# First FFN's down projection computed token-major with 14 seven-product cases, its result turned back on TensorE

## The chip, the cores and the metric

The kernel runs on one core of one Trainium2 chip. The metric is the device time of one execution in microseconds (us). A core has five engines with a queue each, used here as follows: TensorE (PE) for matrix products and transposes, VectorE (DVE) and ScalarE (ACT) for element-wise work, GpSimd (POOL) for a little of it, and SyncE (SP), whose queue issues nearly all DMAs.

## The reference

A decoder trunk of two layers on 256 tokens of width 2048, all in float32. Layer 0 mixes tokens with a gated MLP and attention into 256 memory tokens; layer 1 with latent attention (keys and values from a shared compressed side that is built from x after layer 0) and memory attention. After each mixer stands the same kind of feed-forward network, and at the end one RMSNorm. What matters here is the feed-forward network and what follows it:

```python
def conv_ffn(h, w_up, cw, cb, w_down):
    a = h @ w_up                                   # (256, 2048) @ (2048, 2 * 5632)
    ap = jnp.pad(a, ((0, 0), (CONV_W - 1, 0), (0, 0)))
    c = sum(ap[:, k:k + S] * cw[k] for k in range(CONV_W)) + cb
    gate, val = c[..., :D_FF], c[..., D_FF:]
    return (jax.nn.silu(gate) * val) @ w_down      # (256, 5632) @ (5632, 2048)

for l in range(2):
    if l == 1:
        kv = rmsnorm(x, g_kv) @ w_kv_a             # needs x after layer 0
        ...
    x = x + jnp.concatenate([main, mo], axis=-1) @ w_out[l]
    x = x + conv_ffn(rmsnorm(x, g_ffn[l]), w_ffn_up[l], conv_w[l], conv_b[l], w_ffn_down[l])
return rmsnorm(x, g_final)
```

## The kernel before, in words

**Products.** A float32 number is held as a rounded part hi and a rest lo, and a product is three matmuls: hi x hi, hi x lo and lo x hi. Weights come by DMA into tiles `raw` of 128x1024 (SP's queue), ScalarE makes `whi`, VectorE `wlo` (lines 117 and 118, with a gain per row lines 122 and 123). Activations are kept feature-major: x is `xT`, 16 blocks of 128 features by 256 tokens, its split the tiles `xhl0` and `xhl1`.

**Feature-major products** (`gemm_fm`, line 162): weights are stationary and the 256 tokens move. Four blocks of 128 output features accumulate in four PSUM banks while chunks of 256 rows of the weight pass; a chunk is 24 matmuls of 256 columns (lines 156, 157, 159). Small steps are hung between chunks as hooks: hook n is issued after chunk n.

**The feed-forward network** (`ffn`, line 820) goes in three parts of 4, 4 and 3 groups of 512 inner features. For each group come an up-projection for the gate and one for the value, then convolution, SiLU and product, whose result goes into `h`. After a part's groups comes its down projection. In layer 0 this is feature-major too: four column groups of `gemm_fm` over 16 or 12 blocks of 128 rows; each result is added to x (line 662), and in the last part split for layer 1 and squared on POOL for the norm (`next_operand`, line 672).

**Token-major, in layer 1 only** (class `Tokens`, line 1309, and `down_phase`, line 741): during the second group, x is turned into tokens by VectorE in blocks of 32x32 and 16 DMAs (`turn`). The down projection then has h stationary and 512 weight columns moving, in two phases of 1024 columns. A pair k of two 128-row blocks is a 2x2 block product (two token halves, two column halves), by eight products plainly, and by seven for the pairs that `FF_FAST` (line 34) lists. These need sums of weight blocks (`fast_pair`, line 717, on VectorE) and of h blocks (lines 874 to 890). The listed pairs are three in each phase of parts 0 and 1 and two in the first phase of part 2, 14 in all. A plain pair is 24 matmuls of 512 columns, a seven-product pair 21 (lines 757 to 759). Such a phase holds eight PSUM banks: e00, e01, e10, e11 for the four results and m1, m5, m6, m7 for shared products. ScalarE copies the latter into `staged` (`between`), VectorE adds the e banks to the tokens `xt` (line 1381), and `combine` (six operations, line 1362) adds the shared products: in the next part's first up group, or, in the last part, after the next phase's first addition.

**Order.** The tile framework schedules each engine's instructions by a simulated timeline and may interleave neighbouring stages on PE; `behind` (line 698) chains weight loads and splits of a down phase in program order. After layer 0, `layer_b` (line 1050) starts with the key projection over the 16 blocks of x with the gains g_kv, and forms the norm of x by one matmul of `ssum` against ones (`rstd_bc`, line 267) in hook 3.

Of the kernel before, what the change touches and what calls it, by code (L numbers as in the profile page):

```python
# [8 lines left out]
F32 = mybir.dt.float32  # L9
F32R = mybir.dt.float32r  # L10
# [63 lines left out]
class Kernel:  # L74
# [666 lines left out]
    def down_phase(self, dn, col, order, fast, lhs, rhs, pool, fp, between, evict, finish, late=0, late_gains=None):  # L741
        mm = self.nc.tensor.matmul
# [25 lines left out]
        for n, k in enumerate(order):  # L768
# [16 lines left out]
            else:  # L785
# [33 lines left out]

    def ffn(self, l, after=None, to_tokens=None, tokens=None):  # L820
        nc, t = self.nc, self.t
# [4 lines left out]
        with self.tc.tile_pool(name=self.uid("ff"), bufs=1) as fp:  # L826
            g0 = 0
            for part, ng in enumerate(FF_GROUPS):
                h = self.ap.tile([P, NB * 512], F32R, tag="big", name=self.uid("h"))
                last = part == len(FF_GROUPS) - 1  # L830
                phases = FF_FAST[ng] if tokens is not None else (((), ()), ((), ()))
                fast = phases[0][0]
                if tokens is None:
                    plain = {k: h[:, 1024 * k : 1024 * (k + 1)] for k in range(2 * ng)}
                else:
                    parts7, o = {}, 0
                    for k in fast:
                        n = 896 if k in phases[1][0] else 1024
                        parts7[k] = h[:, o : o + 2 * n].rearrange("p (s q) -> p s q", s=2)
                        o += 2 * n  # L840
                    places = [h[:, i : i + 1024] for i in range(o, NB * 512 - 1023, 1024)]
                    plain = {}
                    for k in range(2 * ng):
                        if k not in fast:
                            plain[k] = places.pop(0) if places else tokens.place()
                block = lambda b: plain[b // 2][:, b % 2 * 512 : (b % 2 + 1) * 512]
# [11 lines left out]
                for g in range(g0, g0 + ng):  # L858
# [34 lines left out]
                    hooks_g, hooks_v = dict(first) if g == 0 else {}, {}  # L893
                    if to_tokens is not None and g == 1:
                        hooks_v = to_tokens
                    if tokens is not None and part and g == g0:
# [3 lines left out]
                if last and l == 0:  # L900
                    self.new_hl()
                dn = down[g0 * 512 : (g0 + ng) * 512]
                g0 += ng
                if tokens is not None:

                    rhs = lambda k, q: tuple(parts7[k][:, i, q * P : (q + 1) * P] for i in range(2))

                    def lhs(k, tb):
                        if k // 2 in parts7:
                            return rhs(k // 2, ((0, 7), (1, 2))[k % 2][tb])  # L910
                        x = block(k)
                        return x[:, tb * P : (tb + 1) * P], x[:, S + tb * P : S + (tb + 1) * P]

                    self.chain = {}
                    for ph in range(2):
                        tokens.begin(ph, last)
                        self.down_phase(
                            dn, 1024 * ph, phases[ph][1], phases[ph][0], lhs, rhs, tokens.pool, fp, tokens.between, tokens.evict, tokens.finish, late=2 if last and ph else 0, late_gains=tokens.gains if last and not ph else None
                        )
                    continue  # L920
# [129 lines left out]
    def layer_b(self):  # L1050
# [9 lines left out]
        with tc.tile_pool(name="lb", bufs=1) as lb:  # L1060
# [235 lines left out]
    def run(self):  # L1296
        nc, tc, t = self.nc, self.tc, self.t
        self.constants()
        with tc.tile_pool(name="mk", bufs=1) as self.mk:
            self.start()  # L1300
            self.layer_a()
        self.ffn(0, lambda j: self.next_operand(j, None))
        self.layer_b()
        with tc.tile_pool(name="fin", bufs=1) as fin:

            Tokens(self, fin).ffn()


class Tokens:
    def __init__(self, kernel, pool):  # L1310
        self.k, self.nc, self.pool = kernel, kernel.nc, pool
        self.xt = pool.tile([P, 2, D], F32, name="xt")
        self.sums = pool.tile([P, 2, 5], F32, name="fsums")
        self.part, self.r, self.q, self.v = (pool.tile([P, 2], F32, name=n) for n in ("fpart", "froot", "fq", "fv"))
        self.staged = None
        self.waiting = []

    def ffn(self):
        turns = {2 * r: [lambda r=r: self.turn(r)] for r in range(4)}
        self.k.ffn(1, to_tokens=turns, tokens=self)  # L1320

# [9 lines left out]
    def place(self):  # L1331
        k = self.k
        self.n = (getattr(self, "n", -1) + 1) % 3
        if self.n < 2:
            tag, o = (("kT1", 32), ("mv1", 0))[self.n]
            return k.cp.tile([P, 1056], F32R, tag=tag, name=k.uid("h" + tag))[:, o : o + 1024]
        return k.tmp(self.pool, [P, 1040], "hx", 1, F32R)[:, 16:]

# [3 lines left out]
    def begin(self, ph, last):  # L1342
        k = self.k
        self.ph, self.last = ph, last
        if ph == 0:
            self.staged = k.ap.tile([P, 2, 4, 512], F32, tag="xT", name=k.uid("staged"))
            if last:
                self.gb = k.ap.tile([P, 2 * D], F32, tag="xhl0", name="gb")[:, :D]

    def gains(self, n):  # L1350
        c = slice(512 * n, 512 * (n + 1))
        g = self.k.t["g_final"].rearrange("(o d) -> o d", o=1)[:, c].to_broadcast([P, 512])
        self.k.behind(self.nc.sync.dma_start(out=self.gb[:, c], in_=g))

# [19 lines left out]

    def evict(self, tb, half, acc, piece=None, meanwhile=lambda: None):
        k, nc, xt, sums = self.k, self.nc, self.xt, self.sums
        j = 2 * self.ph + half
        c0, n = (0, 512) if piece is None else (256 * piece, 256)
        c = slice(j * 512 + c0, j * 512 + c0 + n)
        o = xt[:, tb, c]  # L1380
        add = lambda o, a: nc.vector.tensor_tensor(o, a, o, ALU.add)
        add(o, acc[:, c0 : c0 + n])
        if not self.last:
            return
        if self.ph == 0 and half == 0 and tb == 0:
            for ph in self.waiting:
                self.combine(ph)
            self.waiting = []
        one = lambda x: x[:, tb : tb + 1]
        part, r, q, v, gb = self.part, self.r, self.q, self.v, self.gb  # L1390
# [7 lines left out]
        if piece == 0:  # L1398
            add(xt[:, tb, j * 512 + 256 : (j + 1) * 512], acc[:, 256:])
        meanwhile()  # L1400
# [54 lines left out]
```

## Time and profile before

| | |
|---|---|
| median of 3 runs | 2041.59 us (2041.4 to 2046.97) |
| profiled execution | 2041.58 us |
| its span, first to last instruction | 2039.9 us |
| granted TensorE clock, mean | 0.999 |
| busy: PE, DVE, ACT, POOL | 99%, 73%, 54%, 7% of the span |
| moved by DMA | 394.68 MB, 193 GB/s on average |

The profile comes from one execution. An engine's busy time counts instructions in flight, and matmuls overlap, so the distance between starts tells more than the duration of one. Rows of groups read: line, engine, operation, out<-in, shape, count | busy us, mean ns of one | idle us of the engine before them, and what ended it. Rows of waits read: who waited <- for whom: us in total, times, longest. Rows in order of time begin with start and length in us.

### The profile page before, as it was taken

To read this page: it belongs to the slowest core of one execution; us is meant where nothing else is said; L and a number is where in the kernel's file an instruction comes from. 1 tells how busy PE (TensorE), PEld (TensorE's weight loads), DVE (VectorE), ACT (ScalarE), POOL (GpSimd) and SP (SyncE) were. 2 spreads that over 40 slices of the span, in tenths; PEclk is the share of its full clock that TensorE was granted. 3 is DMA by queue.
4 is the path that set the end of the run, shared out by engine and by line. 5 is a ranking of instruction groups with operands and counts; after the bars stand their busy time and mean duration, and the time that the engine had idled before them with its cause. 6 is when DMAs were issued, how large, how long until landed. Compare 5 with 4: busy or idle time off the path is not lost.

```text
span 2039.9 us, 39921 instructions
## 1 busy us (share of the span) xinstructions
PE 2028.9 (99%) x16232; PEld 1962.7 (96%) x16232; DVE 1496.1 (73%) x2268; ACT 1110.4 (54%) x1605; POOL 142.5 (7%) x200
## 2 busy tenths in 40 slices
PE   9999999999999999999999999999999999999998
PEld 8989999999999999999999999999988999889996
DVE  6866767777656767557778786776878877888777
ACT  6754744555434555345545675454656555555555
POOL 0000013000000000000043142300000000000000
PEclk9999999999999999999999999999999999999999
DMA  8876566666666666666665634668765766557664
GB/s 252 236 215 184 166 191 192 195 194 192 194 197 193 192 195 195 194 193 195 195 194 180 183 112 162 194 192 208 224 204 176 213 194 196 195 187 213 197 212 143
DMA packets 234253, 394.68 MB, mean 193 GB/s; under 512 B 53902, under 2 KB 61396, under 8 KB 234068
## 3 DMA queue, kind: packets, MB, share of 16 engines
q1 hardware_dynamic: 233876, 391.58, 64.0%
q8 instruction: 127, 2.08, 0.4%
q14 instruction: 58, 0.48, 0.1%
q10 hardware_dynamic: 192, 0.54, 0.1%
HBM read 387.88 MB, written 2.10 MB: 191 GB/s over the span
## 4 chain that ended last, share of the span: by engine, by line
PE 98%; DVE 0%; ACT 0%; DMA 0%; issue 0%; SPq 0%; ACTq 0%
PE ps L156 26%; PE ps L157 26%; PE ps L159 26%; PE ps L758 4%; PE ps L759 4%; PE ps L757 4%; PE ps L188 2%; PE ps L189 2%; PE ps L190 2%; PE ps L523 1%; PE ps L603 0%; PE ps L601 0%; PE ps L602 0%; PE ps L1206 0%; DMA raw<-in_w_mem_kv 0%; PE ps L995 0%
## 5 line engine op out<-in xcount | busy, mean ns | idle before, releaser
L118 DVE TENSOR_TENSOR wlo<-raw,whi 128x1024 fp32r<-128x1024 f32 x572 | 710.3, 1245 | 385.0 <-ACT whi L117 380.4
L117 ACT ACTIVATE whi<-raw 128x1024 fp32r<-128x1024 f32 x572 | 607.0, 1062 | 686.6 <-PE ps L157 584.5
L156 PE MATMUL ps<-xhl,whi 128*128 128x256 f32 x3264 | 762.8, 277 | 0.0
L157 PE MATMUL ps<-xhl,whi 128*128 128x256 f32 x3264 | 761.2, 276 | 0.0
L157 PEld LDWEIGHTS ps<-xhl,whi 128*128 128x128 f32 x3264 | 612.9, 188 | 0.4
L156 PEld LDWEIGHTS ps<-xhl,whi 128*128 128x128 f32 x3264 | 612.7, 188 | 0.4
L159 PE MATMUL ps<-xhl,wlo 128*128 128x256 f32 x3264 | 436.5, 276 | 0.0
L159 PEld LDWEIGHTS ps<-xhl,wlo 128*128 128x128 f32 x3264 | 400.4, 188 | 0.0
L156 PE MATMUL ps<-h,whi 128*128 128x256 f32 x704 | 163.6, 276 | 0.0
L157 PE MATMUL ps<-h,whi 128*128 128x256 f32 x704 | 163.6, 276 | 0.0
L157 PEld LDWEIGHTS ps<-h,whi 128*128 128x128 f32 x704 | 132.0, 188 | 0.0
L156 PEld LDWEIGHTS ps<-h,whi 128*128 128x128 f32 x704 | 131.8, 188 | 0.0
L156 PE MATMUL ps<-mainhl,whi 128*128 128x256 f32 x512 | 119.6, 277 | 0.0
L157 PE MATMUL ps<-mainhl,whi 128*128 128x256 f32 x512 | 119.4, 276 | 0.0
L852 ACT ACTIVATE c<-a,cT 128x256 f32<-128x256 f32 x176 | 99.3, 589 | 6.1 <-DVE a L236 6.0
L707 ACT ACTIVATE whi<-raw 128x1024 fp32r<-128x1024 f32 x63 | 66.0, 1059 | 56.5 <-PE ps L759 24.9
L708 DVE TENSOR_TENSOR wlo<-raw,whi 128x1024 fp32r<-128x1024 f32 x63 | 76.5, 1222 | 26.8 <-ACT whi L707 25.9
L157 PEld LDWEIGHTS ps<-mainhl,whi 128*128 128x128 f32 x512 | 96.0, 188 | 0.0
L156 PEld LDWEIGHTS ps<-mainhl,whi 128*128 128x128 f32 x512 | 95.9, 188 | 0.0
L159 PE MATMUL ps<-h,wlo 128*128 128x256 f32 x704 | 94.1, 276 | 0.0
L758 PE MATMUL ps<-wlo,h 128*128 128x512 f32 (+1 forms) x230 | 88.8, 388 | 0.3 <-DVE wlo L708 0.2
L759 PE MATMUL ps<-whi,h 128*128 128x512 f32 (+1 forms) x230 | 88.9, 387 | 0.0
(373 smaller groups left out, 2703.1 us busy)
## 6 DMA issues: line engine op xcount, KB each, us to landing
raw<-in_w_ffn_up SPq DMA_DIRECT2D x352, 512.0 KB, 3.8
raw<-in_w_ffn_down SPq DMA_DIRECT2D x154, 512.0 KB, 4.8
raw<-in_w_out SPq DMA_DIRECT2D x64, 512.0 KB, 4.6
raw<-in_w_in_a SPq DMA_DIRECT2D x56, 512.0 KB, 4.5
raw<-in_w_mem_kv SPq DMA_DIRECT2D x31, 512.0 KB, 4.7
gate<-in_w_ffn_down SPq DMA_DIRECT2D x22, 512.0 KB, 5.9
raw<-in_w_in_b SPq DMA_DIRECT2D x16, 512.0 KB, 4.5
raw<-in_w_kv_a SPq DMA_DIRECT2D x9, 512.0 KB, 5.1
```

What stands on the lines that cost most here:

```text
L117: nc.scalar.activation(hi[:, :n], raw[:, :n], AF.Copy)
L118: nc.vector.tensor_tensor(lo[:, :n], raw[:, :n], hi[:, :n].bitcast(F32), ALU.subtract)
L156: mm(acc[:, :S], wh, x[:, :S], start=first, stop=False)
L157: mm(acc[:, :S], wh, x[:, S:], start=False, stop=False)
L159: mm(acc[:, :S], wl, x[:, :S], start=False, stop=last)
L188: mm(acc, xh, wh, start=first, stop=False)
L707: self.behind(self.nc.scalar.activation(hi, w, AF.Copy))
L708: self.behind(self.nc.vector.tensor_tensor(lo, w, hi.bitcast(F32), ALU.subtract))
L757: mm(o, xh, wh, start=start, stop=False)
L758: mm(o, xh, wl, start=False, stop=False)
L759: mm(o, xl, wh, start=False, stop=stop)
L852: nc.scalar.activation(c, a, AF.Identity, scale=w(2), bias=w(3))
```

## The change

Layer 0's feed-forward network takes the token-major way of layer 1. The class `Tokens` becomes the base of two: `Last` keeps what layer 1 did, and `Inner` serves layer 0. Per part of layer 0:

- the up-projections write h in the form of layer 1, seven sums of blocks for the listed pairs; x is turned into tokens during the second group of layer 0;
- the down projection runs as two calls of `down_phase` with the same `FF_FAST`;
- in the last part, the two phases' results are added into `xt`, and ScalarE squares every 512 columns of a token half with a running sum (`sums`);
- in the second phase of the last part, hooks 1 to 4 turn the finished blocks 0 to 7 of x back to feature-major: four PE transposes for two blocks into one PSUM bank, ScalarE copies hi into `xhl` and x into a new `xT`, VectorE makes lo;
- blocks 8 to 15 are turned in hooks 1 and 2 of layer 1's key projection, and the hook of the norm's matmul goes from 3 to 4;
- `ssum` is no longer summed by POOL; it is the identity times the token's sum of squares, so that the same matmul with ones gives the same row.

The three places for h outside its tile lie in a pool of their own in layer 0, and the tile `we` of the seven-product pairs, in both layers, takes the buffer `src`.

```diff
@@ class Kernel
     def halves(self):
         tiles = [self.ap.tile([P, NB // 2, 512], F32R, tag=f"xhl{i}", name=self.uid("xhl")) for i in range(2)]
+        self.hl_tiles = tiles
...
-        one = self.tmp(pool, [P, 1040], "we", 1, F32R)[:, :1024]
+        one = self.tmp(pool, [P, 1024], "src", 1, F32R)
...
@@ down_phase, at the end of each pair
+            for f in hooks.get(n, ()):
+                f()
...
@@ ffn
-                phases = FF_FAST[ng] if tokens is not None else (((), ()), ((), ()))
+                phases = FF_FAST[ng]
...
+                self.chain = {}
+                for ph in range(2):
+                    extra = tokens.begin(ph, last)
+                    self.down_phase(
+                        dn, 1024 * ph, phases[ph][1], phases[ph][0], lhs, rhs, tokens.pool, fp, tokens.between, tokens.evict, tokens.finish, **extra
+                    )
+                if last:
+                    tokens.done()
-                for j in range(4):
-                    src = self.rows(dn, j * 512, 512)
-
-                    def ed(b, acc):
-                        self.add_residual(4 * j + b, acc)
-                        if last:
-                            after(4 * j + b)
-
-                    self.gemm_fm(src, list(range(4 * ng)), 4, block, ed)
...
@@ layer_b
-            self.gemm_fm(self.rows(wkv, 0, KR), ks, 4, x, ek, gain=gk, hooks={3: [lambda: self.rstd_bc(rb, ssum, D)]})
+            hooks = self.pending | {4: [lambda: self.rstd_bc(rb, ssum, D)]}
+            self.gemm_fm(self.rows(wkv, 0, KR), ks, 4, x, ek, gain=gk, hooks=hooks)
...
@@ run
-        self.ffn(0, lambda j: self.next_operand(j, None))
+        with tc.tile_pool(name="mid", bufs=1) as mid:
+            Inner(self, mid).ffn(0)
...
 class Tokens:
+    places = ("hx0", 0), ("hx1", 0), ("hx2", 0)
...
+    def added(self, tb, half, acc, c0=0, n=512):
         j = 2 * self.ph + half
+        o = self.xt[:, tb, j * 512 + c0 : j * 512 + c0 + n]
+        self.nc.vector.tensor_tensor(o, acc[:, c0 : c0 + n], o, ALU.add)
+        if self.last and self.ph == 0 and half == 0 and tb == 0:
             for ph in self.waiting:
                 self.combine(ph)
             self.waiting = []
+        return j, o
...
+class Inner(Tokens):
+    def begin(self, ph, last):
+        super().begin(ph, last)
+        return {"hooks": {n: [lambda n=n: self.turned(2 * n - 2)] for n in range(1, 5)}} if last and ph else {}
+
+    def evict(self, tb, half, acc):
+        j, o = self.added(tb, half, acc)
+        if self.last:
+            junk = self.quarters()[:, :512]
+            self.nc.scalar.activation(junk, o, AF.Square, accum_out=self.sums[:, tb, j : j + 1])
+
+    def turned(self, k0):
+        k, nc = self.k, self.nc
+        if k0 == 0:
+            k.new_hl()
+            k.x = k.ap.tile([P, NB, S], F32, tag="xT", name=k.uid("xT"))
+
+        def put(b, acc):
+            a = acc.rearrange("p (k s) -> p k s", k=2)
+            hl = k.hl_tiles[b // 8][:, b % 8 : b % 8 + 2, :]
+            nc.scalar.activation(hl[:, :, :S], a, AF.Copy)
+            nc.vector.tensor_tensor(hl[:, :, S:], a, hl[:, :, :S].bitcast(F32), ALU.subtract)
+            nc.scalar.activation(k.x[:, b : b + 2, :], a, AF.Copy)
+
+        k.token_transpose(self.xt, k0, k0 + 2, put)
+
+    def done(self):
+        k, nc = self.k, self.nc
+        total = self.sums[:, :, 4]
+
+        def squares():
+            nc.vector.tensor_reduce(total, self.sums[:, :, :4], AX.X, ALU.add)
+            for tb in range(2):
+                nc.vector.tensor_scalar(k.ssum[:, tb * P : (tb + 1) * P], k.ident, total[:, tb : tb + 1], None, ALU.mult)
+
+        squares()
+        k.pending = {1 + i: [lambda i=i, j=j: self.turned(8 + 4 * i + 2 * j) for j in range(2)] for i in range(2)}
...
+class Last(Tokens):
+    places = ("kT1", 32), ("mv1", 0), ("hx", 0)
...
```

More of the change, by code (lines that the diff above doesn't have):

```diff
@@ L817, in down_phase, with ffn @@
             finish(1)
-    def ffn(self, l, after=None, to_tokens=None, tokens=None):
+    def ffn(self, l, to_tokens, tokens):
         nc, t = self.nc, self.t
@@ L830, in ffn @@
                 last = part == len(FF_GROUPS) - 1
-                phases = FF_FAST[ng] if tokens is not None else (((), ()), ((), ()))
+                phases = FF_FAST[ng]
                 fast = phases[0][0]
[L833 to L845, printed above, removed]
+                parts7, o = {}, 0
+                for k in fast:
+                    n = 896 if k in phases[1][0] else 1024
+                    parts7[k] = h[:, o : o + 2 * n].rearrange("p (s q) -> p s q", s=2)
+                    o += 2 * n
+                places = [h[:, i : i + 1024] for i in range(o, NB * 512 - 1023, 1024)]
+                plain = {}
+                for k in range(2 * ng):
+                    if k not in fast:
+                        plain[k] = places.pop(0) if places else tokens.place()
                 block = lambda b: plain[b // 2][:, b % 2 * 512 : (b % 2 + 1) * 512]
@@ L893, in ffn @@
                     hooks_g, hooks_v = dict(first) if g == 0 else {}, {}
-                    if to_tokens is not None and g == 1:
+                    if g == 1:
                         hooks_v = to_tokens
-                    if tokens is not None and part and g == g0:
+                    if part and g == g0:
                         hooks_g = tokens.deferred()
@@ L1312, in __init__, with hold, ffn @@
         self.xt = pool.tile([P, 2, D], F32, name="xt")
+        self.held = [self.hold(tag) for tag, _ in self.places]
+        for tag, (owner, n) in [(t, h) for (t, _), h in zip(self.places, self.held)] + [("src", (pool, 1024))]:
+            if owner is pool:
+                pool.tile([P, n], F32R, tag=tag, name=kernel.uid(tag), bufs=1)
         self.sums = pool.tile([P, 2, 5], F32, name="fsums")
-        self.part, self.r, self.q, self.v = (pool.tile([P, 2], F32, name=n) for n in ("fpart", "froot", "fq", "fv"))
-        self.staged = None
         self.waiting = []
-    def ffn(self):
+        self.n = 0
+    def hold(self, tag):
+        return self.pool, 1024
+    def ffn(self, l):
         turns = {2 * r: [lambda r=r: self.turn(r)] for r in range(4)}
-        self.k.ffn(1, to_tokens=turns, tokens=self)
+        self.k.ffn(l, turns, self)
     def turn(self, r):
@@ L1342, in begin @@
     def begin(self, ph, last):
-        k = self.k
         self.ph, self.last = ph, last
         if ph == 0:
[L1346 to L1353, printed above, removed]
+            self.staged = self.k.ap.tile([P, 2, 4, 512], F32, tag="xT", name=self.k.uid("staged"))
+        return {}
     def between(self, accs):
@@ new lines, with __init__, hold, begin @@
+class Last(Tokens):
+    places = ("kT1", 32), ("mv1", 0), ("hx", 0)
+    def __init__(self, kernel, pool):
+        super().__init__(kernel, pool)
+        self.part, self.r, self.q, self.v = (pool.tile([P, 2], F32, name=n) for n in ("fpart", "froot", "fq", "fv"))
+    def hold(self, tag):
+        return (self.pool, 1024) if tag == "hx" else (self.k.cp, 1056)
+    def begin(self, ph, last):
+        super().begin(ph, last)
+        if not last:
+            return {}
+        if ph:
+            return {"late": 2}
+        self.gb = self.k.ap.tile([P, 2 * D], F32, tag="xhl0", name="gb")[:, :D]
+        return {"late_gains": self.gains}
+    def gains(self, n):
+        c = slice(512 * n, 512 * (n + 1))
+        g = self.k.t["g_final"].rearrange("(o d) -> o d", o=1)[:, c].to_broadcast([P, 512])
+        self.k.behind(self.nc.sync.dma_start(out=self.gb[:, c], in_=g))
+    def evict(self, tb, half, acc, piece=None, meanwhile=lambda: None):
+        k, nc, xt, sums = self.k, self.nc, self.xt, self.sums
+        c0, n = (0, 512) if piece is None else (256 * piece, 256)
+        j, o = self.added(tb, half, acc, c0, n)
+        c = slice(j * 512 + c0, j * 512 + c0 + n)
+        if not self.last:
+            return
```

51 lines of the change are left out of this document (16 added, 35 removed).

## The prediction

> **What bounds the kernel now.** I read the page from the top, then the waits of TensorE, then its order of time. The first columns of the page give busy time and share of the span; the chain is the work that ended last, followed back.
>
> ```profile
> span 2039.9 us, 39921 instructions
> PE 2028.9 (99%) x16232; PEld 1962.7 (96%) x16232; DVE 1496.1 (73%) x2268; ACT 1110.4 (54%) x1605; POOL 142.5 (7%) x200
> PEclk9999999999999999999999999999999999999999
> PE 98%; DVE 0%; ACT 0%; DMA 0%; issue 0%; SPq 0%; ACTq 0%
> ```
>
> The chain is 98% PE and the clock is granted in full in every slice. The waits of PE are these, and no others:
>
> ```profile
> PE ps L490 <- DVE ones L287: 1.1, 1, 1.1
> PE ps L523 <- ACT memhl L457: 0.7, 1, 0.7
> PE ps L758 <- DVE wlo L708: 0.2, 1, 0.2
> PE ps L603 <- DVE pT L245: 0.2, 1, 0.2
> ```
>
> They sum to 2.2 us of 2039.9. So the time is the work in PE's queue: a matmul less is time gained, a matmul more is time lost, and work on VectorE, ScalarE or GpSimd counts only if it makes PE wait. What a matmul costs is its distance to the next start, not its 276 or 389 ns of busy time, because they overlap. Two answers in order of time give that distance, for groups of 24 matmuls of 256 columns (rows of the last 8 of each group):
>
> ```profile
> 1074.04 1.07 PE L159 MATMUL ps<-xhl,wlo 128*128 128x256 f32 x8
> 1076.76 1.07 PE L159 MATMUL ps<-xhl,wlo 128*128 128x256 f32 x8
> ```
>
> and for the moving operand of 512 columns in layer 1:
>
> ```profile
> 1512.78 0.39 PE L758 MATMUL ps<-wlo,h 128*128 128x512 f32 x1
> 1513.01 0.39 PE L759 MATMUL ps<-whi,h 128*128 128x512 f32 x1
> 1513.23 0.39 PE L758 MATMUL ps<-wlo,h 128*128 128x512 f32 x1
> 1513.46 0.39 PE L759 MATMUL ps<-whi,h 128*128 128x512 f32 x1
> ```
>
> 2.72 us / 24 = 0.1133 us for 256 columns; (1513.46 - 1512.78) / 3 = 0.227 us for 512. The price is by column, so turning the loop from feature-major to token-major gains nothing by itself. Only leaving out products does.
>
> **The change part by part.** *Removed from PE.* Before, part 0 of layer 0 has 8 pairs of row blocks x 4 column groups x 24 = 768 matmuls of 256 columns. After, it is what layer 1 has already: 2 phases x (5 plain pairs x 24 + 3 seven-product pairs x 21) = 366 of 512. Both can be read as stages of this trace. The first two rows are the start and the last eight matmuls of part 0 in layer 0, the others the start and end of the same part in layer 1:
>
> ```profile
> L156 PE MATMUL ps<-h,whi x704: 276/276/276, 528.2 to 1071.1; 128*128 128x256 f32 x176
> 614.36 1.07 PE L159 MATMUL ps<-h,wlo 128*128 128x256 f32 x8
> 1495.53 0.40 PE L757 MATMUL ps<-whi,h 128*128 128x512 f32 x1
> 1578.77 0.40 PE L759 MATMUL ps<-whi,h 128*128 128x512 f32 x1
> 1579.01 0.28 PE L156 MATMUL ps<-xhl,whi 128*128 128x256 f32 x1
> ```
>
> Layer 0: 614.36 + 8 x 0.1133 - 528.2 = 87.07 us. Layer 1: 1579.01 - 1495.53 = 83.48 us, with four 256-column matmuls of the next stage drawn in between (0.47 us): 83.01 us. Difference 4.06 us, of which 18 omitted products x 0.2267 = 4.08 are the reason; the borders between phases cost nothing visible. Part 1 has the same plan: 4.06 again. Part 2 has two seven-product pairs in its first phase only: 6 x 0.2267 = 1.36. Together 14 cases x 3 = 42 matmuls: **-9.48 us**.
>
> *Added to PE.* Eight groups of four transposes of 128x128. The trace has such groups in the memory tokens at the start, 24 matmuls of 256 columns between one and the next:
>
> ```profile
> L405 PE MATMUL ps<-ident,mtok x32: 272/273/371, 4.4 to 26.7; 128*128 128x128 f32 x32
> 22.76 0.62 PE L523 MATMUL ps<-memhl,whi 128*128 128x256 f32 x4
> 23.21 0.60 PE L405 MATMUL ps<-ident,mtok 128*128 128x128 f32 x4
> 23.57 0.71 PE L523 MATMUL ps<-memhl,whi 128*128 128x256 f32 x4
> 26.39 0.60 PE L405 MATMUL ps<-ident,mtok 128*128 128x128 f32 x4
> ```
>
> From one group to the next it is 3.18 us, 2.72 of them matmuls, so a group costs 0.46 (0.36 until the next matmul starts, and 0.10 that the first one after it is late). 8 x 0.46 = **+3.68 us**. From below, with all switches hidden, 8 x 0.35 = 2.8; from above, one transpose at a time between matmuls:
>
> ```profile
> 211.49 0.27 PE L644 MATMUL ps<-ident,mp 128*128 128x128 f32 x1
> 211.52 0.37 PE L156 MATMUL ps<-xhl,whi 128*128 128x256 f32 x1
> 211.73 0.49 PE L644 MATMUL ps<-ident,mp 128*128 128x128 f32 x3
> ```
>
> 0.24 us for one transpose with one matmul, 0.13 above the matmul: 32 x 0.13 = 4.2. I take the group's price, since the code issues them in fours. The sums of squares cost PE nothing new: one matmul against the ones is there before and after, only one chunk later (hook 4 for hook 3).
>
> [...]
>
> *VectorE and ScalarE in the phases.* Columns of the next rows: length, then busy us and instructions of PE, PEld, DVE, ACT, POOL, then the clock.
>
> ```profile
> 528.10:615.20 87.10, 87.10 (x771) 87.10 (x770) 50.20 (x66) 37.41 (x41) 0.00 (x0) 1.00 0.63 194
> 1495.50:1578.60 83.10, 83.10 (x371) 68.90 (x370) 72.14 (x93) 47.76 (x58) 0.00 (x0) 1.00 0.56 190
> 1600.00:1700.00 100.00, 100.00 (x885) 100.00 (x884) 75.23 (x117) 55.73 (x75) 0.00 (x0) 1.00 0.69 197
> ```
>
> The weight sums of the seven-product pairs take VectorE from 50.2 of 87.1 us to 72.1 of 83.1, and PE is still busy throughout. The third row is up-projection in layer 1, with the seven sums of h and the deferred combination in it: 885 matmuls in 100 us, full speed. I cost all of this at nothing, hidden behind PE; the cover that is left is about 11 us in each part. Without it the extra 22 us of VectorE would show.
>
> *The turn of x into tokens* moves into the second up group of layer 0, with 4 transposes on VectorE and 16 DMAs put into SP's queue among the weight loads:
>
> ```profile
> L1325 DVE STREAM_TRANSPOSE xs<-xT x4: 1240/1242/1246, 1380.1 to 1397.0; 128x1024 f32<-128x1024 f32 x4
> L1329 SPq DMA_DIRECT2D xt<-xs x16: 591/664/5072, 1381.5 to 1409.2; - x16
> ```
>
> In layer 1 the same step stands in that place without a wait of PE. Nothing again; uncovered it would be 5 us of VectorE.
>
> *What leaves* (residual additions, splits, the squares on POOL) was beside PE and gains nothing.
>
> *The last phase and the hand-over.* Here the before kernel has no model, so I count. Durations:
>
> ```profile
> L1381 DVE TENSOR_TENSOR xt<-ps,xt 128x512 f32<-128x512 f32 x23 | 15.3, 685 | 7.0 <-PE ps L759 6.9
> L1397 ACT ACTIVATE fjunk<-xt 128x512 f32<-128x512 f32 x7 | 4.4, 626 | 5.6 <-DVE xt L1381 5.0 <-DVE xt L1362 0.6
> L457 ACT ACTIVATE memhl<-ps 128x512 fp32r<-128x512 f32 x8 | 4.8, 595 | 7.2 <-PE ps L405 7.2
> L458 DVE TENSOR_TENSOR memhl<-ps,memhl 128x512 fp32r<-128x512 f32 x8 | 5.5, 690 | 5.9 <-ACT memhl L457 5.9
> L122 ACT ACTIVATE whi<-raw,gT 128x512 fp32r<-128x512 f32 x96 | 63.9, 716 | 42.6 <-PE ps L157 20.4 <-DMA raw<-in_w_mem_kv 12.8 <-issue 7.8
> L123 DVE SCALAR_TENSOR_TENSOR wlo<-raw,gT,whi 128x512 fp32r<-128x512 f32 x96 | 72.7, 794 | 19.5 <-ACT whi L122 19.5
> 1995.11 0.39 PE L759 MATMUL ps<-we,h 128*128 128x512 f32 x1
> 2004.55 1.22 DVE L1362 TENSOR_TENSOR xt<-xt,staged 128x1024 f32<-128x1024 f32 x1
> ```
>
> The first transposes need the combination of the phase before. In layer 1 it ended at 2005.8, and the last product with the tile we, which closes that phase, started at 1995.11; the hook stands two pairs, 48 x 0.227 = 10.9 us, into the next phase, at 2006.2 on that scale. The cover is 0.4 us, and 0.7 more because layer 0 lacks the multiplication by the final gains that stands in between; four transposes held up there would hold up all of PE behind them. At the end, PE goes into the first four chunks of the key projection, 4 x 2.72 = 10.9 us, with operands turned earlier; the second half of x is needed in chunk 4. ScalarE must do meanwhile four squares (3.3 us with the reads of the sums), eight copies from PSUM (4.8) and the weights (1.43 a chunk, 5.7): 13.8 us against 10.9, plus the 4 us before the end in which the first accumulators are already whole. VectorE: four additions (2.7), four subtractions (2.8), weights (1.6 a chunk, 6.4): 11.9. Both just fit, and four buffers of weights lie ahead. Queued behind a late copy on ScalarE would be the next weights, and PE waits for those. From below nothing; from above the 2.9 us by which ScalarE exceeds the four chunks. I take 0.2, near the other borders of phases.
>
> Sum against the profiled execution of 2041.58 us (span 2039.9 and 1.7 around it; the median of the three runs is 2041.59): 2041.58 - 9.48 + 3.68 + 0.2 = **2036.0 us**.
>
> **The rivals.**
> *Hand-over late.* Copies and squares hold ScalarE and PE waits once or twice, or the first transposes reach PE before the combination is done. For it: the two ledgers above are nearly full. Against: the weights lie ahead. 1.5 to 4 us: 2037.5 to 2040.
>
> *Transposes not pipelined.* If each waits for the one before, 32 x 0.273 = 8.7 us: 2041.0. [...]
>
> *Slower: accumulators.* A seven-product phase holds all eight PSUM banks, and the next phase needs banks that four additions of 0.685 must free. If PE stands at the border until they are done, that is 2.74 us, at five borders and the hand-over 16.4: 2052. It decides for slower from 5.6 / 6 = 0.93 us a border, and for slower by more than 0.3% from 2.0. Layer 1 has the same five borders, and there PE waited 0.2 us in all.
>
> *The products are omitted but PE gains nothing,* because weight sums come late on VectorE and PE runs at its pace: then the transposes alone remain, 2045. Against: part 0 of layer 1 took 83.01 us.
>
> *Transposes hidden* under a 512-column stream, 2.8 us or less: 2034.5 or below. For it only that no group of this trace stands in such a stream.
>
> **How the numbers follow.** The forecast, 2034.5 to 2037.5, has 0.64; late hand-over 0.16; transposes not pipelined 0.04; accumulators 0.07; no gain on PE 0.04; transposes hidden 0.05. The range 2034.5 to 2040.0 holds the first two, 0.80; its ends are also the bounds of the unknown costs (2.8 for the transposes and no wait give 2034.9; 4.2 with a wait of 2.9 gives 2039.2). 0.3% of the median is 6.1 us, about what a measurement of this kernel can tell from no change. Faster by more than that is below 2035.5: the hidden transposes and a quarter of the forecast, 0.22. Slower: the accumulators and a little of the no-gain case, 0.08. The rest, 0.70, lies between: I expect a gain of 0.27%.
>
> **What would show it.** Right: part 0 of layer 0 takes 83.0 us from its first product of h to its last, likewise part 1; PE's waits stay within a microsecond of 2.2 in all; each group of transposes moves the next matmul by 0.46. Wrong: waits of PE on VectorE at L757 to L759 in layer 0 (accumulators or weight sums), on xhl or whi in the first chunks of the key projection (hand-over), or a distance above 0.15 us from transpose to transpose.

## The result and the profile after

The changed kernel takes 2035.9 us in the median of 7 runs (2035.36 to 2037.23) against 2041.59 before: a ratio of 0.9968 with a 95% interval of 0.9956 to 0.998. The forecast was 2036.0. The head of the page after:

```profile
span 2035.5 us, 37928 instructions
PE 2025.5 (100%) x15166; PEld 1919.8 (94%) x15166; DVE 1572.9 (77%) x2373; ACT 1149.6 (56%) x1661; POOL 112.7 (6%) x169
PE 99%; DVE 0%; ACT 0%; issue 0%; ACTq 0%
```

Nothing changed in kind: the chain is PE, VectorE has 77 us more to do and POOL 30 less. The waits of PE after, all of them:

```profile
PE ps L490 <- DVE ones L287: 1.1, 1, 1.1
PE ps L759 <- DVE wlo L709: 0.2, 1, 0.2
PE ps L603 <- DVE pT L245: 0.2, 1, 0.2
```

Not one is new. To see where the time went, take two places that the change does not touch, and their first start in each trace: the first product of layer 0's output projection (mainhl) and of layer 1's queries (qhl). Rows of line 156, before and then after:

```profile
L156 PE MATMUL ps<-mainhl,whi x512: 275/276/467, 266.6 to 1319.8; 128*128 128x256 f32 x171
L156 PE MATMUL ps<-qhl,whi x72: 276/276/282, 1154.3 to 1218.8; 128*128 128x256 f32 x72
```

```profile
L156 PE MATMUL ps<-mainhl,whi x512: 275/276/468, 268.0 to 1315.6; 128*128 128x256 f32 x171
L156 PE MATMUL ps<-qhl,whi x72: 276/276/283, 1150.1 to 1214.6; 128*128 128x256 f32 x72
```

Between them lies everything that was changed: 1154.3 - 266.6 = 887.7 us before, 1150.1 - 268.0 = 882.1 after, **5.6 us less**. What follows is alike, 885.6 and 885.4 us to the end of the span. The 1.4 us by which mainhl starts later belong to the start of this one execution, read below; they fit the profiled run (2037.23) being the slowest of the seven. I call the stretch from mainhl to qhl the changed stretch and use it for every kernel.

Inside it, parts 0 and 1 of layer 0 after the change: the start of part 0 and of the stage behind it, and a window over each part, as long as the one that the prediction laid over layer 1's part 0 (length, then busy us and instructions of PE, PEld, DVE, ACT and POOL, then the granted clock):

```profile
529.60 0.40 PE L758 MATMUL ps<-whi,h 128*128 128x512 f32 x1
613.08 0.28 PE L156 MATMUL ps<-xhl,whi 128*128 128x256 f32 x1
```

```profile
529.50:612.60 83.10, 83.10 (x371) 68.91 (x370) 72.11 (x94) 47.76 (x58) 0.00 (x0) 1.00 0.56 190
786.70:869.80 83.10, 83.10 (x371) 68.90 (x371) 72.11 (x93) 47.75 (x58) 0.00 (x0) 1.00 0.56 190
```

From the first product of h to the next stage it is 83.48 us, with four 256-column matmuls of that stage drawn in (0.47): 83.0 us, as the prediction worked it out for layer 1. The windows agree with layer 1's: 371 matmuls in 83.1 us in both parts, 72.1 us with VectorE busy, PE without a gap. And the transposes, in the last phase and in the key projection:

```profile
1042.56 0.60 PE L405 MATMUL ps<-ident,xt 128*128 128x128 f32 x4
1042.92 1.18 PE L758 MATMUL ps<-whi,h 128*128 128x512 f32 x4
1043.93 0.60 PE L405 MATMUL ps<-ident,xt 128*128 128x128 f32 x4
...
1070.76 1.08 PE L159 MATMUL ps<-xhl,wlo 128*128 128x256 f32 x8
1071.67 1.04 PE L405 MATMUL ps<-ident,xt 128*128 128x128 f32 x8
1074.38 1.07 PE L159 MATMUL ps<-xhl,wlo 128*128 128x256 f32 x8
```

A four delays the next matmul by 0.36 us, as at the start of the kernel, and four matmuls after it took 1.01 instead of 0.91: 0.46 in all. Two fours in one hook run as one eight: from one chunk's last eight matmuls to the next chunk's it is 1074.38 - 1070.76 = 3.62, 0.90 above the 2.72 of a chunk.

### The profile page after: what moved, and what is told of

It reads as the page before. It is cut to its first block, busy times and chain, and to the rows that moved or that the text cites. A ratio compares the mean times of both kernels' runs of the same rounds, so it can differ in the third digit from the quotient of the medians.

```text
span 2035.5 us, 37928 instructions
## 1 busy us (share of the span) xinstructions
PE 2025.5 (100%) x15166; PEld 1919.8 (94%) x15166; DVE 1572.9 (77%) x2373; ACT 1149.6 (56%) x1661; POOL 112.7 (6%) x169
## 4 chain that ended last, share of the span: by engine, by line
PE 99%; DVE 0%; ACT 0%; issue 0%; ACTq 0%
PE ps L156 22%; PE ps L157 22%; PE ps L159 22%; PE ps L759 7%; PE ps L760 7%; PE ps L758 7%; PE ps L188 2%; PE ps L189 2%; PE ps L190 2%; PE ps L523 1%; PE ps L405 0%; PE ps L603 0%; PE ps L601 0%; PE ps L602 0%; PE ps L1195 0%; PE ps L983 0%
## 5 line engine op out<-in xcount | busy, mean ns | idle before, releaser
L117 ACT ACTIVATE whi<-raw 128x1024 fp32r<-128x1024 f32 x484 | 513.0, 1062 | 524.7 <-PE ps L157 417.6
L118 DVE TENSOR_TENSOR wlo<-raw,whi 128x1024 fp32r<-128x1024 f32 x484 | 598.9, 1241 | 265.7 <-ACT whi L117 261.7
L709 DVE TENSOR_TENSOR wlo<-raw,whi 128x1024 fp32r<-128x1024 f32 x126 | 152.8, 1221 | 55.0 <-ACT whi L708 53.2
L708 ACT ACTIVATE whi<-raw 128x1024 fp32r<-128x1024 f32 x126 | 131.9, 1058 | 111.8 <-PE ps L760 48.9
L760 PE MATMUL ps<-whi,h 128*128 128x512 f32 (+1 forms) x458 | 177.5, 388 | 0.0
L759 PE MATMUL ps<-wlo,h 128*128 128x512 f32 (+1 forms) x458 | 177.2, 389 | 0.3 <-DVE wlo L709 0.2
L758 PE MATMUL ps<-whi,h 128*128 128x512 f32 (+1 forms) x458 | 154.3, 389 | 0.0
L708 ACT ACTIVATE whi<-xs 128x1024 fp32r<-128x1024 f32 x56 | 59.0, 1060 | 83.0 <-PE ps L760 48.0
L759 PEld LDWEIGHTS ps<-wlo,h 128*128 128x128 f32 x458 | 86.0, 188 | 18.4 <-DVE wlo L709 1.2
L760 PEld LDWEIGHTS ps<-whi,h 128*128 128x128 f32 x458 | 86.0, 188 | 17.5
L758 PEld LDWEIGHTS ps<-whi,h 128*128 128x128 f32 x458 | 85.9, 188 | 17.4
```

Of the source, the lines that this page charges most:

```text
L117: nc.scalar.activation(hi[:, :n], raw[:, :n], AF.Copy)
L118: nc.vector.tensor_tensor(lo[:, :n], raw[:, :n], hi[:, :n].bitcast(F32), ALU.subtract)
L708: self.behind(self.nc.scalar.activation(hi, w, AF.Copy))
L709: self.behind(self.nc.vector.tensor_tensor(lo, w, hi.bitcast(F32), ALU.subtract))
L758: mm(o, xh, wh, start=start, stop=False)
L759: mm(o, xh, wl, start=False, stop=False)
```

## The experiments

The theory: PE's columns decide, 0.227 us for each omitted product of 512 columns and some 0.46 for each four transposes; everything else is hidden while it fits behind PE. The rivals were that the gain comes from the work taken off VectorE and POOL at the end of layer 0, that the transposes cost something else, and that the hand-over or VectorE's weight sums are a bound. Times are medians; the kernel before took between 2041.48 and 2041.94 beside them. Each edit is against the changed kernel unless another is named.

**e1_no_seven: the seven-product cases undone alone.**

```diff
-                phases = FF_FAST[ng]
+                phases = FF_FAST[ng] if l else (((), tuple(range(2 * ng))),) * 2
```

> Layer 0's down projections stay token-major with the transposes back, but all pairs are plain: the 42 omitted products return. Theory (PE's columns alone decide): 42 x 0.2267 = 9.5 us more than the changed kernel, about 2045.4 us, that is 3.7 to 3.9 above the kernel before, the price of eight groups of transposes; part 0 takes 87.0 us. Rival (the gain comes from what was taken off VectorE and POOL at the end of layer 0, not from the products): no more than a few us above 2036 and below the kernel before.

Measured 2045.34 us, 1.0016 of the kernel before (1.0007 to 1.0026). The row of line 156 for qhl, and for mainhl:

```profile
L156 PE MATMUL ps<-mainhl,whi x512: 275/276/467, 266.3 to 1323.7; 128*128 128x256 f32 x171
L156 PE MATMUL ps<-qhl,whi x72: 276/276/282, 1158.1 to 1222.6; 128*128 128x256 f32 x72
```

The changed stretch is 891.8 us: 9.7 more than with the products omitted, 4.1 more than before. So token-major with transposes and without omitted products is slower than the kernel it replaces, and the relief of POOL and VectorE is worth nothing that shows. The first rival has fallen.

**e2_twice: the transposes doubled.**

```diff
-                for tb in range(2):
+                for tb in list(range(2)) * times:         # times is 2: token halves 0, 1, 0, 1
...
-        k.token_transpose(self.xt, k0, k0 + 2, put)
+        k.token_transpose(self.xt, k0, k0 + 2, put, 2)
```

> Each of the 32 transposes of x is issued twice into the same place of PSUM. Theory (transposes are pipelined, 0.0875 us from start to start inside a group, the switch paid once per group): 32 x 0.0875 = 2.8 us more than the changed kernel, about 2038.7 us. Rival (each waits for the one before, 0.273 us): 8.7 us more, 2044.6. Rival (hidden beside the 512-column stream): under 1 us.

Measured 2039.23 us, 3.3 more than the changed kernel (0.9985 of before, 0.9976 to 0.9994). Groups of eight and sixteen:

```profile
1040.81 1.04 PE L405 MATMUL ps<-ident,xt 128*128 128x128 f32 x8
1041.60 1.17 PE L758 MATMUL ps<-whi,h 128*128 128x512 f32 x4
...
1071.65 1.91 PE L405 MATMUL ps<-ident,xt 128*128 128x128 f32 x16
1073.32 0.36 PE L156 MATMUL ps<-xhl,whi 128*128 128x256 f32 x1
```

Eight delay the next matmul by 0.79 us against 0.36 for four: 0.11 for each further one, not the 0.0875 that I had from dividing a four by four, and far from 0.273. The theory holds with that size corrected: 32 x 0.107 = 3.4.

**e3_pool_squares: the norm's sum undone alone.**

```diff
-            nc.scalar.activation(junk, o, AF.Square, accum_out=self.sums[:, tb, j : j + 1])
...
             nc.scalar.activation(k.x[:, b : b + 2, :], a, AF.Copy)
+            for j in (b, b + 1):
+                k.square_add(k.ssum, k.x[:, j, :], j == 0, k.cp)
...
-        squares()
```

> One part undone: the norm's squares are formed on POOL from the blocks that were turned back, as in the kernel before, and not on ScalarE from the token rows. Theory (the sum must be ready at chunk 4 of the key projection, some 16 us after the last phase, where its matmul holds PE's queue): POOL needs 0.8 + 1.2 us a block, 16 us for the second eight blocks from about 1074 us on, against 1081.6 where the matmul stands: PE waits 8 to 10 us, about 2045 us. Rival (the norm is not on the path and ScalarE's squares cost as much as they save): within 1 us of the changed kernel.

Measured 2039.11 us, 3.2 more than the changed kernel (0.9984, 0.9974 to 0.9993). Neither fits: it is a third of what I expected and three times the rival's 1 us. PE's order there shows why:

```profile
1087.79 0.96 PE L159 MATMUL ps<-xhl,wlo 128*128 128x256 f32 x7
1090.57 0.70 PE L269 MATMUL ps<-ssum,ones 128*128 128x256 f32 x2 [1.83 <-POOL ssum L279]
...
1095.90 1.12 PE L159 MATMUL ps<-xhl,wlo 128*128 128x256 f32 x8
1098.78 1.12 PE L159 MATMUL ps<-xhl,wlo 128*128 128x256 f32 x8
```

POOL took some 17 us for the second eight blocks, 2.6 of them for other work, but the scheduler did not leave the norm's matmul behind chunk 4. It put it behind the key projection, at 1090.57, where PE waited 1.83 us. I had priced a wait at the place where the code has it, and the schedule had moved it. The changed stretch is 884.9 us, 2.8 more than the changed kernel's. The rest, about 1 us, goes with chunks that start 2.88 us apart behind the wait instead of 2.72; why, at a granted clock of 0.999 over the run, stays open. So the squares on ScalarE are worth some 3 us of the change: with them on POOL, more than half of the gain would be gone.

**e4_four_first: a fourth seven-product pair a phase in layer 0.**

```diff
+FF_FOUR = {4: (((1, 2, 3, 4), (0, 1, 5, 2, 6, 3, 7, 4)), ((1, 2, 3, 4), (0, 1, 5, 2, 6, 3, 7, 4))), 3: FF_FAST[3]}
...
-                phases = FF_FAST[ng]
+                phases = FF_FAST[ng] if l else FF_FOUR[ng]
```

> Layer 0 takes four seven-product pairs a phase in parts 0 and 1 instead of three, 18 cases instead of 14. Theory (PE's columns decide as long as VectorE has cover, 11 us a part, of which the fourth pair takes 7.3): 4 x 3 x 0.2267 = 2.7 us less than the changed kernel, about 2033.2 us, with PE's waits under 1 us. Rival (VectorE becomes the bound, 79.4 us of 81.6 a part and uneven): PE waits for wlo, no gain or a loss of some us.

Measured 2047.13 us, 11.2 more than the changed kernel (1.0025, 1.0015 to 1.0035). The rival's sign, but not its reason. PE's waits in part 0 with ScalarE's order before the first of them, SP's longest wait in that time, SP's order, and windows with the clock (then the share of DMA and GB/s):

```profile
547.17 0.73 PE L761 MATMUL ps<-whi,h 128*128 128x512 f32 x2 [2.85 <-ACT whi L711]
549.25 1.22 PE L761 MATMUL ps<-whi,h 128*128 128x512 f32 x2 [1.06 <-ACT whi L711]
```

```profile
546.06 1.06 ACT L711 ACTIVATE whi<-gate 128x1024 fp32r<-128x1024 f32 x1 [3.96 <-DMA gate<-in_w_ffn_down]
```

```profile
SPq L779 <- DVE hv L874: 16.2, 1, 16.2
```

```profile
525.06 16.95 SPq L779 DMA_DIRECT2D gate<-in_w_ffn_down  x2
542.42 0.80 SPq L779 DMA_DIRECT2D raw<-in_w_ffn_down  x2
```

```profile
535.00:545.00 10.00, 9.32 (x42) 7.38 (x40) 7.08 (x13) 3.63 (x7) 0.00 (x0) 1.00 0.22 54
545.00:555.00 10.00, 6.77 (x17) 4.98 (x18) 8.83 (x10) 5.59 (x6) 0.00 (x0) 0.66 0.75 259
```

Read backwards: PE waits for weights that ScalarE rounds late, because their load came late. In the first phase the weights of the listed pairs behind the first go into tiles `gate`. The second listed pair is now pair 2, fourth in the order, where the changed kernel has pair 3, sixth in the order. So its load meets `gate` while the last up group still holds it for its products hv: SP's queue stood for 16.2 us, and the plain weights queued behind stood with it, at 54 GB/s in the window before. VectorE was busy 7.08 of 10 us meanwhile. Then the clock: 0.66 in the second window means 6.8 us at half speed. About 1.0 of them is the second wait itself; the 14 matmuls from 549.25 to 555.25 took 6.00 us in place of 14 x 0.227 = 3.2, so the clock cost 2.8. Part 1 shows the same (waits of 2.72 and 1.06 us). Waits of 7.7 us and 2 x 2.8 lost to the clock, less the 2.7 gained, are 10.6; measured 11.2, and 11.5 in the changed stretch. The last half to one microsecond stays open.

**e5_raw_first and e6_raw_both: that load moved to free tiles.** e5 is e4 with this line changed, e6 has `FF_FOUR` in both layers, 18 cases in each (the 22 in its expectation is a slip).

```diff
-                if k in fast and (col or k != fast[0]):
+                if k in fast and (col or k not in fast[: max(1, len(fast) - 2)]):
                     raw = self.tmp(fp, [P, 1024], "gate", 2)
```

> As e4_four_first (four seven-product pairs a phase in parts 0 and 1 of layer 0), but the weights of the second listed pair, too, go into tiles raw in the first phase, and not into a tile gate that the last up group still holds. Theory (e4 lost its time because the load into gate stood 16 us in SP's queue until gate was free, PE then waited 4 us a part and ran 7 us at half clock): no wait above 0.3 us in the parts, 4 x 3 x 0.2267 = 2.7 us less than the changed kernel, about 2033.2 us. Rival (VectorE's weight sums are the bound with four pairs a phase): waits of PE on wlo or whi stay, above 2036.

> The same four pairs a phase in both layers, 22 cases in each order of parts instead of 14 (18 a layer instead of 14). Theory: twice the gain of e5, 5.4 us less than the changed kernel, about 2030.5 us. Rival (VectorE bound in layer 1, where the tail has more for it to do): between 2031 and 2036.

Measured 2033.38 us for e5 (0.9956, 0.9942 to 0.9971), 2.5 less than the changed kernel, and 2031.44 for e6 (0.9945, 0.9929 to 0.9961). Every wait of PE at the down projections is gone but one in layer 1 that was there before (0.2 us). The changed stretch of e5 is 879.3 us, 2.8 below 882.1. That settles e4: it was the buffer and not VectorE. The median of e6 lies in its rival's range, since it is 1.9 below e5 where 2.7 were expected; but behind the changed stretch its trace is 882.8 us long against 885.4 in e5, 2.6 less, and no wait is added. VectorE was nearly full at times without making PE wait, as a window of e6 in layer 1 shows (DVE 19.93 of 20 us, PE 20.00):

```profile
1520.00:1540.00 20.00, 20.00 (x90) 16.57 (x89) 19.93 (x25) 13.42 (x17) 0.00 (x0) 1.00 0.62 209
```

**e7_hook0: the hand-over tightened.**

```diff
-        k.pending = {1 + i: [lambda i=i, j=j: self.turned(8 + 4 * i + 2 * j) for j in range(2)] for i in range(2)}
+        k.pending = {0: [lambda j=j: self.turned(8 + 2 * j) for j in range(4)]}
```

> The last 16 transposes stand right behind the first chunk of the key projection instead of behind the second and third. Theory (the hand-over has cover: additions are over some 1.5 us after the last product of the phase, the first chunk takes 2.7): at most 1 us of wait, and PSUM banks for four groups at once are missing, so some waiting on the copies; within 1.5 us of the changed kernel, 2036 to 2037.5. Rival (the hand-over is the tight place): 3 us or more, and a stretch at a lower clock.

Measured 2035.91 us (0.9969, 0.9957 to 0.9982), the changed kernel's time. Sixteen transposes now stand behind the first chunk:

```profile
1066.26 1.07 PE L159 MATMUL ps<-xhl,wlo 128*128 128x256 f32 x8
1067.17 1.91 PE L405 MATMUL ps<-ident,xt 128*128 128x128 f32 x16
1070.75 1.07 PE L159 MATMUL ps<-xhl,wlo 128*128 128x256 f32 x8
```

From chunk to chunk it is 4.49 us, 1.77 for sixteen, and no wait. The hand-over has a whole chunk of cover, 2.7 us, to spare, so its rival has fallen.

**e8_sums5: more work for VectorE in the parts.** In layer 0 the last weight sum of every listed pair is formed five more times into the same place.

```diff
         add(t24[:, right], t24[:, left], y[:, left])
+        for _ in range(self.extra):                       # 5 in layer 0, 0 in layer 1
+            add(t24[:, right], t24[:, left], y[:, left])
```

> In layer 0 every seven-product pair repeats the last of its four weight sums five times into the same place: 14 x 5 x 0.685 = 48 us more work on VectorE, 20.6 us in each of parts 0 and 1, against about 11 us that it had idle there. Theory (VectorE's work is free only up to its cover): PE waits some 10 us in each of the two parts, less what spills into the neighbouring stages, and 6.8 us beside it in part 2: 2045 to 2065 us, with stretches of lower clock. Rival (the cover is not the idle share, since loads and buffers run ahead): within 2 us of the changed kernel.

Measured 2065.45 us, 29.6 more (1.0112, 1.0094 to 1.0131), half a microsecond above the range expected. PE's waits in the parts, a window about the second of them, and the instruction of ScalarE that ended that wait:

```profile
PE ps L762 <- ACT whi L708: 18.4, 9, 3.6
```

```profile
556.00:562.00 6.00, 4.26 (x19) 3.19 (x18) 5.97 (x7) 3.90 (x4) 0.00 (x0) 1.00 0.40 128
```

```profile
557.36 2.01 ACT L708 ACTIVATE whi<-xs 128x1024 fp32r<-128x1024 f32 x2 [6.04 <-DVE xs L724]
```

Beyond the cover VectorE does bind: it was busy for 5.97 us of 6, and ScalarE stood for 6.04 us until VectorE had formed the sums that it rounds. The waits add up to 18.4 us, 8.5 in part 0, 7.1 in part 1 and 2.9 in part 2; four stretches of 3.4 us at half clock (0.72 to 0.74 granted over the 6 us about each) came on top, worth 1.7 each, an estimate by half their length. That is 25 of the 28.5 us by which the changed stretch grew; the rest stays open. In parts 0 and 1 the idle share was a fair measure of the cover: 7.3 us more in e5 cost nothing, 20.6 cost some 8 of waiting. In part 2 it was not, as two windows of the changed kernel show, one over the start of its first phase and one over the whole part:

```profile
1000.40:1012.00 11.60, 11.60 (x54) 9.59 (x53) 11.49 (x23) 6.64 (x12) 0.00 (x0) 1.00 0.46 158
1000.40:1066.00 65.60, 65.60 (x300) 54.31 (x299) 53.58 (x73) 39.55 (x62) 0.00 (x0) 1.00 0.56 185
```

VectorE had 12.0 us idle there and got 6.8 more, yet PE waited 2.9, from 11.5 us into the phase on: the idle time lies behind the place where the sums are needed, and before it VectorE was already busy for 11.49 of 11.60 us. Idle time counts as cover only where it lies ahead of the instruction that waits.

**e9_third_part2, e10_third_raw and e11_third_early: a third listed pair in part 2, both layers.** Each is an edit of the one before it, e9 of e6.

```diff
# e9
-3: FF_FAST[3]}
+3: (((1, 2, 4), (0, 1, 3, 2, 5, 4)), ((), (0, 1, 2, 3, 4, 5)))}
# e10
-                if k in fast and (col or k not in fast[: max(1, len(fast) - 2)]):
+                if k in fast and (col or k not in fast[:2]):
# e11
-3: (((1, 2, 4), (0, 1, 3, 2, 5, 4)),
+3: (((1, 2, 3), (0, 1, 4, 2, 5, 3)),
```

> As e6_raw_both, and in both layers the first phase of part 2 has three seven-product pairs instead of two: 19 cases a layer. Theory (PE's columns decide while VectorE and the loads keep up): 2 x 3 x 0.2267 = 1.4 us less than e6, about 2030.0 us. Rival (part 2 is short, its sums of weights stand in 33 us with the phase before and the combination behind): PE waits a microsecond or more at L761, no gain, 2031.4 or above.

> As e9_third_part2, but in the first phase of part 2, too, the weights of the second listed pair go into tiles raw. Theory (e9 lost its time by the wait of 2.9 us a layer for a load that stood 9 us in SP's queue until gate was free, and by the half clock behind it): no wait at L761, the 1.4 us that e9 was to bring below e6, about 2030.0 us. Rival (VectorE's sums are the bound in the short part): a wait of a microsecond or more stays, 2031.4 or above.

> As e10_third_raw, but the third listed pair of part 2 is pair 3, made in the second up group, and not pair 4, made in the last. Theory (in e9 and e10 the tile we of the first listed pair had to wait until the sums of h for pair 4, made just before, had left the one buffer src that both share since the change): no wait of PE at L761 in part 2, 1.4 us below e6, about 2030.0 us. Rival (VectorE's weight sums are the bound in the short part): a wait of some 3 us a layer stays, about 2040.

e9 took 2039.62 us (0.9986, 0.9977 to 0.9996), e10 2040.01 (0.999, 0.9981 to 1.0). In e9 PE waited 2.9 us a layer in part 2, with half clock behind each wait (in layer 0 0.74 granted from 1000 to 1010 us, 0.91 in the 10 us after), and SP's queue had again stood for `gate`, 9.1 us. I took that for the cause, and e10 refuted it: nothing stood behind `gate` any more, and the wait was the same. ScalarE's order in e10 just before PE's wait:

```profile
1002.63 1.06 ACT L892 ACTIVATE h<-src 128x1024 fp32r<-128x1024 f32 x1 [1.26 <-DVE src L889]
1003.59 0.70 ACT L247 ACTIVATE hhx<-hv 128x256 fp32r<-128x256 f32 x2
1004.98 0.63 ACT L711 ACTIVATE src<-raw 128x512 fp32r<-128x512 f32 x1 [0.68 <-DVE h L893]
1005.52 1.99 ACT L711 ACTIVATE whi<-xs 128x1024 fp32r<-128x1024 f32 x2
```

The third row is the tile `we` of the first listed pair, which since the change takes the single buffer `src`. The first row reads the same buffer: it holds the seven sums of h for pair 4, formed in the last up group, and `we` can only be written when VectorE has read those (line 893), and the weights of the pair come behind it. With pair 3, whose sums are made a group earlier, e11 took **2028.56 us**, 0.9935 (0.9919 to 0.9952), the best of all: 7.3 us below the changed kernel and 12.9 below the one before beside it. No wait at L761 is left; the rival, VectorE's weight sums, has fallen. The edit moves the work of pair 4's sums away together with their hold on `src`, so that the shared buffer alone is the cause is read from the order above and not shown by a run. The lead on e6 is 2.9 us in the medians, where 1.4 were expected. In the profiled executions it is 0.9 in the changed stretch (878.6 us against 879.5) and 0.2 behind it, where a new wait of 0.6 us at an up-projection of layer 1 takes most of that layer's gain. Half a microsecond of the medians' lead lies in the kernel before as well (2041.94 beside e6, 2041.48 beside e11); the rest stays open, with four runs of each.

## Why the prediction was right

*Removed from PE, -9.48.* Right. The two kernels with and without the omitted products differ by 9.4 us in the median and 9.7 in the changed stretch; part 0 took 83.0 us as layer 1's did.

*Added to PE, +3.68.* Right: the group price of 0.46 held for fours (0.46) and eights (0.90), 3.64 us in all. In the changed stretch e1, which has everything but the omitted products, is 4.1 us above the kernel before; the other half microsecond is not located. The distance inside a group was mis-sized, 0.11 for 0.0875, as e2 shows. The last transpose of the four at 1042.56 tells why:

```profile
1042.89 0.27 PE L405 MATMUL ps<-ident,xt 128*128 128x128 f32 x1
```

The four start 0.11 us apart, but the matmul behind them, at 1042.92, starts only 0.03 after the last: 3 x 0.11 + 0.03 = 0.36, and a fourth of that is too little for one more transpose. The lower bound of 2.8 was therefore no bound but out of reach.

*VectorE and ScalarE at nothing.* Right, by the row: 72.11 of 83.10 us, no wait. e5 and e8 place the bound: 7 us more a part are still free, 21 are not.

*The turn of x at nothing.* No wait of PE stands at it. No run took it away by itself.

*The hand-over, 0.2 us.* There was no wait, and e7 shows that one chunk of cover was left beyond what the code uses. My ledgers, which called it nearly full, counted ScalarE's copies of x, at which no wait of PE stands, as if the next chunk needed them. For the first transposes I had 0.4 to 1.1 us of cover. The combination, which follows the first addition of its own phase and not of the next, ended at 1039.2, and the transposes started at 1042.56, 3.4 us later.

*The rivals.* Accumulators: PE waited at none of the five borders. Transposes not pipelined: e2. Transposes hidden: e2, and the 0.46 of each four in a stream of 512 columns. No gain on PE: e1. The late hand-over: e7. Measured by e1, the forecast's sum takes off 0.2 too little, adds 0.4 too little and has 0.2 for a wait that did not come; these cancel, so that the distance of 0.1 us from the median is partly luck. The terms are good to about half a microsecond.

## What to carry to other kernels

When PE has no waits, price a change in columns of its queue, and take the stage price from a place where the kernel does the same thing already. A new tenant of a buffer is the risk: ask which earlier stage still holds it, and which queue stands while it is held; in e4 one tile turned a gain into a loss of 11.2 us, and e10 lost 8.6 us against e6 where, by ScalarE's order, another was held. Before pricing a wait by its place in the code, ask whether the scheduler may move the instruction that waits.

## What the hardware showed that was not expected

**A short wait can cost more than itself.** In e8, waits of 3.56 us (ending at 572.5), 1.92 (602.6), 2.12 (841.6) and 2.88 (1036.6) each came with about 3.4 us at half clock, in which matmuls of 512 columns start 0.43 us apart in place of 0.227, while waits of 1.25, 1.74 and 1.95 (871.7) did not. So length alone does not decide: 1.92 us did and 1.95 did not. Here are the 3.41 us that hold the wait of 1.92 us, and the 3.41 us behind them, and the same for the wait of 1.95:

```profile
600.21:603.62 3.41, 1.49 (x7) 0.93 (x6) 3.38 (x5) 2.11 (x3) 0.00 (x0) 1.00 0.09 18
603.62:607.03 3.41, 3.41 (x9) 2.67 (x8) 3.41 (x4) 1.91 (x2) 0.00 (x0) 0.50 0.82 294
869.86:873.27 3.41, 1.56 (x7) 1.30 (x8) 3.41 (x4) 2.67 (x3) 0.00 (x0) 1.00 0.21 49
873.27:876.68 3.41, 3.41 (x17) 2.80 (x16) 3.41 (x4) 2.30 (x3) 0.00 (x0) 1.00 0.69 258
```

The wait of 1.92 us lies whole in the first row, where PE was busy for 1.49 us, and the second has half clock, 0.50. Of the wait of 1.95, 1.85 us lie in the third row, where PE was busy for 1.56 us, and in the fourth the clock stays at 1.00. What decides between the two is not shown. A stretch at half clock in which PE still waited 1.00 us (e4) or 0.74 (e9) lasted about 6.8 us; one with 0.26 us (e10, at 1970.5) lasted about 3.4.

**The start varies by over a microsecond.** In the profiled execution of the changed kernel, PE's first matmuls are slow for longer than in that of before (first transposes of the memory tokens, before and then after):

```profile
11.86 0.60 PE L405 MATMUL ps<-ident,mtok 128*128 128x128 f32 x4
```

```profile
9.02 1.05 PE L405 MATMUL ps<-ident,mtok 128*128 128x128 f32 x4
13.19 0.60 PE L405 MATMUL ps<-ident,mtok 128*128 128x128 f32 x4
```

After, four transposes still take 1.05 us at 9.02, and the third group comes 1.33 us later, an offset that stays to the end. Over the thirteen traces the first product on mainhl starts between 266.2 and 268.0 us. For differences of a few microseconds, compare stretches inside the traces, and medians of several runs, not one span with another.
